# Class keys only of blocks outside the local scores, counted in the local masks; five products on a constant fewer; a fixed order at four other places

## The chip, the cores and the metric

The kernel runs on one core of one Trainium2 chip, in one launch. The metric is the device time of that launch in microseconds (us). A core has a matrix engine (TensorE, PE in the profile, with its weight loads as PEld), a vector engine (VectorE, DVE), an activation engine (ScalarE, ACT), a general engine (GpSimd, POOL) and a sync engine (SP) that issues the DMA transfers. Each engine works through its own queue in order; semaphores hold an instruction back until what it reads is there.

## The reference

One decoder layer on x of 1024 tokens by 1024 features, float32, with two mixers whose outputs are concatenated:

```python
h = rmsnorm(x, norm1_w)
proj = h @ w_in
# mixer A: gated delta rule, 4 heads of 128, gated by silu(z)
# mixer B: dilated attention, 8 heads of 64
DIL_PATTERNS = ((128, 1), (512, 4), (2048, 16))
...
for window, dil in DIL_PATTERNS:
    # query t sees keys t, t-dil, ..., t-window
    num, den, m = band_attention(stride(qf), stride(kf), stride(vf), window // dil)
...
out = num_tot / den_tot            # branches weighted by their softmax denominators
...
x = x + concat([o_a, o_b]) @ w_out
h = rmsnorm(x, norm2_w)
u = causal_dwconv(h @ w_up, ffn_conv_w)
x = x + (silu(gate) * up) @ w_down
return rmsnorm(x, final_norm_w)
```

The merge of the three attention branches amounts to one softmax over all keys of the query, in which a key that several branches see counts as often as they see it. Branch 1 sees the last 128 tokens. Branches 2 and 3 see only keys whose distance is a multiple of 4 (up to 512) or of 16.

## The kernel before, in words

Float32 matrices are split into a rounded high part and the rest (a low part), and a product of two of them is three products: high by high, high by low, low by high (`mm3`, L196, "a group" below). ACT makes the high part, DVE the low part (`split`, L202). Everything lies transposed: features or weights on the partitions, tokens along the row.

A planner writes the program: streams of work (`wv.add`, L1603) yield their estimated due times, and `Weave.run` decides in which order PE's products are recorded. PE keeps that order. On the other engines a scheduler orders what is recorded; `after(inst, anchor)` (L185) fixes that one instruction stands behind another, and `uv` and `ua` are DVE and ACT with a higher priority.

- **Start (L261 to L346).** Eighteen products on a constant tile `warm` come first (L332). Then `first()` computes three column blocks of the input projection: for each k of eight feature blocks, six groups (three blocks by two token halves). A tile of x per k is loaded, split into `xhi` and `xlo`, squared and summed into `acc` for the first norm. For k = 0 the tile comes in two halves, and the groups take all three blocks of one half first. Weights for two k at a time are loaded and split (`whi`, `wlo`); the adds for the norm stand in the same DVE queue.
- **Mixer A (to about 300 us)** and the rest of the input projection (`dense`, L486): 16 groups per column block, eight for each token half, with the result scaled by `rstdB` into `xr` or `aqkv` by DVE. The dense groups fill PE between the steps of the other streams. The z columns come last; `gate` (L463) makes silu(z) times the mixer's output `og` from them.
- **Attention (L879 to L1036).** Two heads (e = 0, 1, on 64 partitions each) at a time make a head pair, `pi` = 0 to 3; eight query blocks n of 128 tokens each, in pairs: (0, 1), (2, 3), (4, 5), (6, 7). Inside a block, tokens are ordered by class, that is, by position modulo 4. For a block, `scores` computes *local scores*, against its own and the previous block (128 columns for n = 0, 256 otherwise), and *class scores*: each of the four classes against the keys of the same class, of `nb` blocks of class keys, 128 columns per `nb`. `nb` is 1 for n < 4 and 2 from n = 4 on. A class product has 32 stationary columns, so four classes and two heads make eight per block. Masks from the tiles `mks` add a large negative number, or the logarithm of the count, to each column; a row's exponentials and sum follow (`normalise`, L930). `turn` transposes the probabilities on PE, 128 columns at a time; DVE copies the local part to `pt`, ACT the class part to `pb`. `values` multiplies by local values, and `merge_classes` (L975), once for four blocks, by class values: for each class, class-key block and head one product of 128 columns (four blocks of 32 queries). `give` copies the result `oT` out. The pairs are pipelined by one: a pair's scores are recorded before the values of the pair before it.
- **Output projection (L1073).** Its products start when attention is over and the last z is gated; `mixer_splits` splits `og` into `ohi`, `olo`.
- **Up projection (L1187 to L1320).** Seven half-size products P1 to P7 per step instead of eight, for 22 steps. P1, P6, P7 and P4 add up in one bank `pa`, of which ACT takes copies on the way (`p1`, `u2`, `u3`), so that the next product waits for the copy. In the first step the second norm is also computed: row sums on PE, a power on POOL (`rms2_power`, L1171), transposes of the result and a copy to `rstdB` (`rms2_spread`, L1180).
- **Down projection (L1326 to L1601).** Stages 0 to 3 of 11 steps each; each step's operands are prepared one or two steps ahead (`prep`, L1384, DVE's part in `lows`), ACT and DVE in the order written down (`keep`, L1351). In stage 3 the right half of the tokens is already done and is normed (`final_norm`, L1517: row sums, `rs`, a power on POOL, four transposes, eight scalings with their output transfers); its two steps `down_step(3, 4)` and `(3, 5)` lie between the row sums and the transposes. The last five steps are run column block by column block in products of 256 columns, so that the left half's norm can be done in two quarters.

Of the kernel before, what the change touches and what calls it, by code (L numbers as in the profile page):

```python
# [144 lines left out]
def hybrid_layer(tc, I, out):  # L145
# [126 lines left out]

    for k in range(KT):
# [24 lines left out]
        sq = A("sq", "qa")  # L298
        ac.activation(sq, xt, AF.Square)
        if k == 0:  # L300
            sq0 = sq
        elif k == 1:
            ve.tensor_tensor(acc, sq0, sq, op=OP.add)
        else:
            inst = ve.tensor_tensor(acc, acc, sq, op=OP.add)
            if k == 6:
                after(inst, first_lo, "the products wait for these weights")
        if k == 4:
            first_lo = wlast

# [21 lines left out]
    for _ in range(18):  # L332
        mm(wbank[:, :P], warm, warm, 0.3)
# [129 lines left out]
    def gate(og, xr, anchor=None):  # L463
# [3 lines left out]
                 ve.tensor_tensor(og, og, y, op=OP.mult)]  # L467
        if anchor is not None:
# [409 lines left out]

    def attention():  # L879
# [11 lines left out]
        def mask(n):  # L891

            i, o, step, w, m = {0: (0, 128, 352, 128, 2), 1: (1, 0, 128, 128, 3), 2: (1, 384, 128, 128, 3),
                                3: (0, 608, 128, 128, 3)}.get(n, (0, 0, 480 - 32 * n, 256, 2))
# [3 lines left out]
        def scores(pair):  # L898
# [76 lines left out]
        def merge_classes(g):  # L975
# [41 lines left out]
        for pi in range(4):  # L1017
            q, k, vn, vc = cur
            for hh in range(2):
# [9 lines left out]
                for u in (0, 2):  # L1029
                    more = att_values(qkv[2]) if (hh, u) == (1, 2) and pi < 3 else None  # L1030
                    yield from advance([dict(n=4 * hh + i, u=i, q=q, k=k, vn=vn, nb=nb, po=po, pb=pb, g=g)
# [16 lines left out]
    def mixer_splits():  # L1048
# [4 lines left out]
        for i in range(8):  # L1053
            yield from wv.until(("o", i))
            ots[i] = (X("ohi"), X("olo"))
            if i < H:
                split(gated[i], *ots[i])
# [79 lines left out]
    def split_block(b, src):  # L1137
        ac.activation(b[0], src, AF.Copy)
        return ve.tensor_tensor(b[1], src, b[0].bitcast(F32), op=OP.subtract)

    def residual(m):
# [11 lines left out]
        else:  # L1153
# [8 lines left out]
            split_block(hblock("T4", i), b21)  # L1162
            split_block(hblock("B22", i), b22)
        for h in range(2):
# [6 lines left out]
    def rms2_power():  # L1171
# [4 lines left out]
        ve.tensor_scalar(rs, ps[:, :NCH], 1.0 / 1024, EPS, op0=OP.mult, op1=OP.add)  # L1176
# [20 lines left out]
    def up_weights(n, names):  # L1197
# [18 lines left out]
        if "A22" in names:  # L1216
# [7 lines left out]
            split_block(pairs[1], u)  # L1224
            for i, name in enumerate(("S3", "A12", "S4", "A22")):
# [17 lines left out]
    def up(n, before):  # L1243
# [16 lines left out]
        ac.activation(u2, pa, AF.Copy)  # L1260
# [6 lines left out]
        if before is not None:  # L1267
# [3 lines left out]
        ac.activation(u3, pa, AF.Copy)  # L1271
# [4 lines left out]
        if before is None:  # L1276
            rms2_spread(rs)
# [239 lines left out]
    def final_norm(hh, sl, tags, between=None, more=()):  # L1517
# [9 lines left out]
        ve.tensor_scalar(rs[:, :n_], ss[:, :n_], 1.0 / 1024, EPS, op0=OP.mult, op1=OP.add)  # L1527
        rsqrt(rs[:, :n_], rs[:, :n_], n_)
        if between is not None:
            between()  # L1530
        pb = bank(tags[1])
        for c in range(n_):
            tp(pb[:, c * P:(c + 1) * P], rs[:, c:c + 1].to_broadcast([P, P]))
        for m in range(8):
            x = x1h[m][:, part(m, hh, sl)]
            ve.scalar_tensor_tensor(x, x, fw[:, m:m + 1], pb[:, :sl.stop - sl.start], op0=OP.mult, op1=OP.mult)
# [139 lines left out]
```

## Time and profile before

| | us |
|---|---|
| median of 3 timed runs | 1232.29 |
| lowest, highest | 1231.43, 1234.54 |
| profiled execution, its own time | 1235.56 |
| its span, first to last instruction | 1233.3 |
| PE busy in it | 1215.4 |

The page gives the busy time of each engine; a share near 100% for PE means that the stage's length is the sum of its products, as long as they follow on one another. Rows of groups read: line, engine, operation, out<-in, shapes, count of records | busy us, mean ns | idle time before them and what ended it. A float32 product of PE appears as two records, a transpose as one. A record's mean duration overlaps with its neighbours; busy time does not count the overlap twice. Rows of the timeline read: start, duration, engine, line, operation, out<-in, shapes, count, and in brackets the idle time of the engine before it and what ended it. Rows by stretches read: from:to, length, then busy time and count for each engine asked for, the granted clock, the DMA share and GB/s.

### The profile page before, as it was taken

The numbers are of one execution on the slowest core, as the hardware profiler recorded it, in microseconds if no ns is written. First come the engines' busy times: TensorE is split into PE (matmuls) and PEld (weight loads), VectorE is DVE, ScalarE is ACT, GpSimd is POOL, SyncE is SP. The second block draws the span as 40 slices with busy tenths as digits, with TensorE's granted clock in tenths as the row PEclk, the third lists the DMA queues.
The fourth block names the chain that finished last, engine by engine and source line by source line (L and its number), as shares of the span: only waits on it lengthen the run. The fifth ranks groups of instructions, "written<-read, shape, count | busy, mean of one in ns | idle before, by whom it ended". The sixth has DMA issues, their size and how long they took to land.

```text
span 1233.3 us, 18302 instructions
## 1 busy us (share of the span) xinstructions
PE 1215.4 (99%) x7048; PEld 1005.1 (81%) x7048; DVE 967.1 (78%) x1529; ACT 585.5 (47%) x1127; POOL 51.2 (4%) x34
## 2 busy tenths in 40 slices
PE   9999999999999999999999999999999999999996
PEld 7888887898777777888788888888888888888886
DVE  7686984473666777677789888898898979898986
ACT  7383344363444445455454454454444554445451
POOL 0212110022000000000000000000000000000001
PEclk9999999999999999999999999999999999999999
DMA  7423235337442222443331322312213296357733
GB/s 231 103 75 98 86 115 160 103 103 235 133 132 75 104 61 61 140 162 109 112 103 52 103 85 69 103 57 98 101 54 103 77 358 237 106 183 224 238 95 137
DMA packets 81702, 153.52 MB, mean 124 GB/s; under 512 B 21552, under 2 KB 32464, under 8 KB 81616
## 3 DMA queue, kind: packets, MB, share of 16 engines
q1 hardware_dynamic: 81616, 152.37, 37.9%
q8 instruction: 55, 0.90, 0.3%
q14 instruction: 31, 0.25, 0.1%
HBM read 114.31 MB, written 35.93 MB: 122 GB/s over the span
## 4 chain that ended last, share of the span: by engine, by line
PE 94%; DVE 3%; issue 1%; ACT 1%; DMA 0%; POOL 0%; POOLq 0%; DVEq 0%; ACTq 0%
PE ps L189 46%; PE pa L189 19%; PE dw L189 15%; PE pc L189 9%; PE ps L193 4%; DVE x1h L139 1%; DVE pr L139 1%; PE warm L189 1%; DMA wst<-in_wu 0%; DVE rstdB L139 0%; POOL rs L139 0%; DVE olo L139 0%; DVE pt L141 0%; DVE T L139 0%; DVE wst L139 0%
## 5 line engine op out<-in xcount | busy, mean ns | idle before, releaser
L189 PE MATMUL dw<-pr 128*128 128x512 f32 (+1 forms) x984 | 211.3, 376 | 0.0
L189 PEld LDWEIGHTS dw<-pr 128*128 128x128 f32 x984 | 176.6, 188 | 33.6
L189 PE MATMUL ps<-xhi,whi 128*128 128x512 f32 x448 | 187.0, 417 | 0.0
L189 PE MATMUL ps<-xhi,wlo 128*128 128x512 f32 x448 | 176.1, 393 | 0.0
L189 PE MATMUL ps<-xlo,whi 128*128 128x512 f32 x448 | 175.4, 391 | 0.0
L189 PE MATMUL pa<-T,pair 128*128 128x512 f32 x528 | 127.1, 390 | 2.2 <-ACT u L139 2.2
L189 PEld LDWEIGHTS pa<-T,pair 128*128 128x128 f32 x528 | 98.9, 188 | 23.2 <-ACT u L139 2.7
L189 PEld LDWEIGHTS ps<-xhi,wlo 128*128 128x128 f32 x448 | 84.3, 188 | 18.6
L189 PEld LDWEIGHTS ps<-xhi,whi 128*128 128x128 f32 x448 | 84.5, 189 | 17.1 <-issue 3.3
L189 PEld LDWEIGHTS ps<-xlo,whi 128*128 128x128 f32 x448 | 84.8, 189 | 13.2
L139 ACT ACTIVATE u<-pa 128x512 f32<-128x512 f32 x44 | 26.3, 598 | 108.6 <-PE pa L189 108.6
L139 DVE SCALAR_TENSOR_TENSOR y<-xu,fcw,y 128x1023 f32<-128x1023 f32 (+1 forms) x44 | 56.4, 1281 | 24.4 <-ACT y L139 24.4
L139 ACT ACTIVATE pr<-wd 128x1024 fp32r<-128x1024 f32 x33 | 35.0, 1061 | 76.9 <-DVE wd L139 38.2
L139 ACT ACTIVATE whi<-wst 128x1024 fp32r<-128x1024 f32 (+2 forms) x38 | 38.5, 1014 | 60.0 <-PE ps L189 49.8
L189 PE MATMUL pa<-B,A 128*128 128x512 f32 x264 | 63.5, 389 | 0.0
L189 PE MATMUL pc<-B,pair 128*128 128x512 f32 x264 | 63.4, 389 | 0.0
L189 PE MATMUL pc<-T,S 128*128 128x512 f32 x264 | 63.4, 389 | 0.0
L189 PE MATMUL pa<-T,S 128*128 128x512 f32 x264 | 63.4, 389 | 0.0
L141 ACT ACTIVATE sm<-sm,mx 128x512 f32<-128x512 f32 (+2 forms) x64 | 41.2, 646 | 42.2 <-DVE mx L141 42.2
L139 DVE TENSOR_TENSOR wst<-wst 128x512 f32<-128x512 f32 x88 | 60.3, 686 | 0.7
L189 PE MATMUL ps<-B,pair 128*128 128x512 f32 x252 | 60.5, 389 | 0.0
L189 PEld LDWEIGHTS pa<-T,S 128*128 128x128 f32 x264 | 49.5, 188 | 10.3
(233 smaller groups left out, 2312.5 us busy)
## 6 DMA issues: line engine op xcount, KB each, us to landing
wst<-in_wu SPq DMA_DIRECT2D x44, 512.0 KB, 3.7
wd<-in_wd SPq DMA_DIRECT2D x44, 512.0 KB, 4.4
wst<-in_wi SPq DMA_DIRECT2D x25, 512.0 KB, 3.7
upark<-y SPq DMA_DIRECT2D x22, 512.0 KB, 3.7
r<-upark SPq DMA_DIRECT2D x22, 512.0 KB, 9.3
apark<-aqkv SPq DMA_DIRECT2D x12, 512.0 KB, 2.8
wa<-in_wd SPq DMA_DIRECT2D x22, 256.0 KB, 3.0
wst<-in_wo SPq DMA_DIRECT2D x8, 512.0 KB, 4.1
```

The costliest lines, as they stand in the source:

```text
L139: return getattr(eng, op)(*a, **kw)
L141: return getattr(eng, op)(*a, **kw)
L189: tc.stamp_issue_order_token(nc.tensor.matmul(dst, lhs, rhs, start=start, stop=stop, **kw).ins, TOKEN)
L193: tc.stamp_issue_order_token(nc.tensor.transpose(dst, src, ident).ins, TOKEN)
```

## The change

- **Class keys.** `CBLOCKS` gives each query block its own `nb`: 0 for blocks 0 and 1, 1 for blocks 2 to 5, 2 for blocks 6 and 7. Where a class key lies inside the local 256 columns only, it is no longer a column of its own; the local mask counts how often the three branches see it. The masks are laid out anew. Blocks 0 and 1 have no class scores, no class probabilities and one transpose less per head; blocks 4 and 5 have 128 class columns less. `merge_classes` leaves the blocks without a class-key block out of its products (64 columns instead of 128).
- **Start.** Thirteen products on the constant instead of 18. The x tile of k = 1 is loaded and split in two halves, its groups take one half first, and the squares of a tile are recorded after the split of the next.
- **End of attention.** The gate products and low parts of mixer A's outputs are ordered behind the last copies of probabilities and the low parts of the first output weights.
- **First steps of the up projection.** The copies `u2` and `u3` are ordered ahead of some splits; `rms2_spread` is recorded between P7 and P4 instead of after P4; the sum's scaling has the higher priority.
- **Stage 3 of the down projection.** `rs` and a copy of it behind the power stand in the written DVE order, one step earlier; one step lies between the row sums and the transposes, the other behind them; the eight scalings are ordered behind the last step's low parts.
- **Last norm.** Two of the scalings are ordered behind the adds of the last two column blocks.

```diff
+    def squares(k):
+        sqs[k] = A("sq", "qa")
+        ac.activation(sqs[k], xts[k], AF.Square)
+        if k == 1:
+            ve.tensor_tensor(acc, sqs[0], sqs[1], op=OP.add)
+        elif k > 1:
+            inst = ve.tensor_tensor(acc, acc, sqs[k], op=OP.add)
...
-            sy.dma_start(xt, I["xT"][k * P:(k + 1) * P, :])
+            parts = [half(0), half(1)] if k == 1 else [slice(0, S)]
+            for sl in parts:
+                sy.dma_start(xt[:, sl], I["xT"][k * P:(k + 1) * P, sl])
...
-            split_x(xt, k, slice(0, S))
+            for sl in parts:
+                split_x(xt, k, sl)
+            squares(k - 1)
...
-    for _ in range(18):
+    for _ in range(13):
         mm(wbank[:, :P], warm, warm, 0.3)
...
-            for i in range(6) if k else (0, 2, 4, 1, 3, 5):
+            for i in range(6) if k > 1 else (0, 2, 4, 1, 3, 5):
...
+    CBLOCKS = (0, 0, 1, 1, 1, 1, 2, 2)
...
-                for c in range(4):
+                for c in range(4 if it["nb"] else 0):
...
-            if it["g"]["pi"] == 3 and it["n"] > 5:
-                for lo in last.get("wlo", ()):
+            if it["g"]["pi"] == 3 and it["n"] == 7 and e == 1:
+                lows = last.get("wlo", [])
+                last["probabilities"] = inst
+                for lo in lows:
                     after(lo, inst, "the probabilities go first")
-            ua.activation(it["pb"][e][:, it["u"]].rearrange("p b t -> p (b t)"), pp[:, n1_:wd], AF.Copy)
+                for slow in last["og"] + last.get("olo", [])[1:]:
+                    after(slow, (lows or [inst])[0], "the first weights go first")
+            if it["nb"]:
+                ua.activation(it["pb"][e][:, it["u"], :it["nb"]].rearrange("p b t -> p (b t)"), pp[:, n1_:wd], AF.Copy)
...
+                    us = slice(2 if b == nb - 1 else 0, 4)
                     for e in range(2):
                         er = slice(64 * e, 64 * e + 64)
-                        mm(po[er].rearrange("p (u t) -> p u t", u=4)[:, :, 32 * c:32 * c + 32],
-                           vcv[:, c, b, er], g["pb"][e][:, :, b, 32 * c:32 * c + 32], 0.14,
+                        mm(po[er].rearrange("p (u t) -> p u t", u=4)[:, us, 32 * c:32 * c + 32],
+                           vcv[:, c, b, er], g["pb"][e][:, us, b, 32 * c:32 * c + 32], 0.14 if us.start == 0 else 0.08,
...
+                if i and "probabilities" in last:
+                    after(lo, last["probabilities"], "the probabilities go first")
...
-        ve.tensor_scalar(rs, ps[:, :NCH], 1.0 / 1024, EPS, op0=OP.mult, op1=OP.add)
+        uv.tensor_scalar(rs, ps[:, :NCH], 1.0 / 1024, EPS, op0=OP.mult, op1=OP.add)
...
+            if n == 1:
+                after(last["hi"], last["u3"], "the next product waits for the copy")
...
-        ac.activation(u2, pa, AF.Copy)
+        inst = ac.activation(u2, pa, AF.Copy)
+        if before is None:
+            for hi in last["lasts"]:
+                after(hi, inst, "the next product waits for the copy")
...
         yield from up_product(n, "P7", pa, False, False)
-        if before is not None:
+        if before is None:
+            rms2_spread(rs)
+        else:
             pd = yield from next_bank("hf")
...
         rsqrt(rs[:, :n_], rs[:, :n_], n_)
+        if hh:
+            keep("vector", inst)
+            rp, rs = rs, tile_(sp, [P, 4], F32, "rs3", "rs3", 2)
+            keep("vector", ve.tensor_copy(rs, rp))
...
-                def two_steps():
-                    down_step(3, j)
-                    prep(3, j + 3)
-                    down_step(3, j + 1)
-                final_norm(1, whole, ("hf", "ch"), two_steps)
-            elif stage < 3 or j < HT - LAST - 1:
+                outs = final_norm(1, whole, ("hf", "ch"), lambda: down_step(stage, j))
+            elif stage < 3 or j < HT - LAST:
                 down_step(stage, j)
+        for inst in outs:
+            after(inst, prev["vector"], "the last steps' weights go first")
...
+        after(outs[4], adds[2, right.start], "the last norm waits for it")
+        after(outs[7], adds[3, right.start], "the last norm waits for it")
...
-    p1 = np.where((d >= 0) & (d <= 128), 0.0, NEG)
+    def logs(mult):
+        return np.where(mult > 0, 8.0 * np.log(np.maximum(mult, 1)), NEG)
+    local = logs(((d >= 0) & (d <= 128)).astype(int) + ((d >= 0) & (d % 4 == 0)) + ((d >= 0) & (d % 16 == 0)))
```

More of the change, by code (lines that the diff above doesn't have):

```diff
@@ L271, in split_x @@
                                 op1=OP.subtract)
+    def squares(k):
[5 more added lines that the diff above has]
+            inst = ve.tensor_tensor(acc, acc, sqs[k], op=OP.add)
+            if k == 6:
+                after(inst, first_lo, "the products wait for these weights")
+    sqs = {}
     for k in range(KT):
@@ L293, in hybrid_layer @@
                 sy.dma_start(wst, I["w0"][k // 2])
-            sy.dma_start(xt, I["xT"][k * P:(k + 1) * P, :])
+            parts = [half(0), half(1)] if k == 1 else [slice(0, S)]
+            for sl in parts:
+                sy.dma_start(xt[:, sl], I["xT"][k * P:(k + 1) * P, sl])
             if k % 2 == 0:
                 wlast = split(wst, whi, wlo)
-            split_x(xt, k, slice(0, S))
[L298 to L307, printed above, removed]
+            for sl in parts:
+                split_x(xt, k, sl)
+            squares(k - 1)
         if k == 4:
             first_lo = wlast
+    squares(KT - 1)
     ident = const("ident", [P, P], I["ident"])
@@ L467, in gate @@
                  ve.tensor_tensor(og, og, y, op=OP.mult)]
+        last["og"] = insts[2:]
         if anchor is not None:
@@ L1056, in mixer_splits @@
             if i < H:
-                split(gated[i], *ots[i])
+                lo = split(gated[i], *ots[i])
+                last.setdefault("olo", []).append(lo)
+                if i and "probabilities" in last:
+                    after(lo, last["probabilities"], "the probabilities go first")
             else:
@@ L1275, in up @@
         ac.activation(xu[:, half(0)], pa, AF.Copy)
-        if before is None:
-            rms2_spread(rs)
         def rest():
@@ L1591, in last_product @@
                 down(pa[i], i, ops[3, j][0], sl, False, j == HT - 1)
-            add_to(pa[i], 4 + i, 0, sl)
+            adds[i, sl.start] = add_to(pa[i], 4 + i, 0, sl)
             return complete(4 + i, 0, sl, alone)
@@ L1599, in mlp_down @@
         last_product(0, right)
-        final_norm(0, left, ("hf", "ch"), lambda: last_product(1, right))
-        final_norm(0, right, ("hf", "ch"), more=[last_product(i, right, True) for i in (2, 3)])
+        outs = final_norm(0, left, ("hf", "ch"), lambda: last_product(1, right))
+        squares = [last_product(i, right, True) for i in (2, 3)]
+        after(outs[4], adds[2, right.start], "the last norm waits for it")
+        after(outs[7], adds[3, right.start], "the last norm waits for it")
+        final_norm(0, right, ("hf", "ch"), more=squares)
     wv.add(0, norms())
```

32 lines of the change are left out of this document (19 added, 13 removed).

## The prediction

> **What bounds the kernel now.** I read the busy time by engine first, then the list of who waited for whom on TensorE (PE).
>
> ```profile
> PE 1215.4 (99%) x7048; PEld 1005.1 (81%) x7048; DVE 967.1 (78%) x1529; ACT 585.5 (47%) x1127; POOL 51.2 (4%) x34
> ...
> PE ps L193 <- POOL rs L139: 2.3, 2, 1.2
> ```
>
> PE lacks 17.9 us of the 1233.3 us span. A removed product is therefore worth its full time wherever PE does not stand waiting at that place; work taken from VectorE (DVE) or ScalarE (ACT) is worth nothing by itself. The list of waits is short (its longest entry is above: microseconds in all, times, the longest); those that the new orders touch are quoted at their parts. In the attention stage the same is seen by stretches (sums per engine in one stretch of time):
>
> ```profile
> 375.00:420.00 45.00, 45.00 (x434) 35.54 (x433) 30.82 (x81) 18.90 (x53) 0.00 (x0) 1.00 0.32 105
> ```
>
> PE is busy all 45.00 us, DVE 30.82 of them.
>
> **Part 1, the start.** Thirteen products on a constant are issued instead of 18; each is two records. PE by stretches over those records, then the rows that limit what follows:
>
> ```profile
> 1.10:6.10 5.00, 4.99 (x23) 1.00 0.65 175
> 6.10:7.54 1.44, 1.44 (x15) 1.00 0.90 237
> ...
> 5.21 0.75 DVE L139 SCALAR_TENSOR_TENSOR xlo<-xt,n,xhi 128x512 fp32r<-128x512 f32 x1 [0.50 <-ACT xhi L139]
> 8.78 0.56 DVE L139 TENSOR_TENSOR wlo<-wst,whi 128x384 fp32r<-128x384 f32 x1 [0.61 <-ACT whi L139]
> 10.31 1.28 DVE L139 SCALAR_TENSOR_TENSOR xlo<-xt,n,xhi 128x1024 fp32r<-128x1024 f32 x1 [0.97 <-ACT xhi L139]
> 23.17 0.95 DVE L139 TENSOR_TENSOR wlo<-wst,whi 128x768 fp32r<-128x768 f32 x1
> 24.43 0.39 PE L189 MATMUL ps<-xhi,wlo 128*128 128x512 f32 x1
> ```
>
> Of the 36 records 23 fall in the first 5.00 us (0.22 us each); the 13 left take 1.44 us, 0.11 us each. The ten that go come from the fast end: 10 x 0.11 = 1.1 us, not ten times the mean of 6.44/36 = 0.18. [...]
>
> The operands are there: the low part of the first half of x ends at 5.96, and PE would now ask at 7.54 - 1.1 = 6.4. The next limit is the low weights of k=4. DVE works without a pause from 10.31 to 24.12, when they end, and PE reads them at 24.43, a margin of 0.31. With the second x tile in halves, DVE can begin it at about 9.4 (after the row at 8.78). The order of squares and the halves then cost it about 0.35, and the load of the gate weights, now behind a weight load in the sync queue, perhaps 0.2. So those weights come at about 23.6 and PE asks at 23.3: 0.3 is lost, and I take 0.8. Bounds: 0 and 1.1.
>
> **Part 2, class keys.** Groups of records by form:
>
> ```profile
> L189 PE MATMUL ps<-kT,qT 64*32 64x256 f32 x256 | 8.8, 382 | 0.0
> L189 PE MATMUL ps<-kT,qT 64*32 64x128 f32 x256 | 5.3, 275 | 0.0
> L189 PE MATMUL ps<-pb,vc 128*64 128x128 f32 x192 | 12.0, 273 | 0.0
> L189 PE MATMUL ps<-kT 128*128 128x128 f32 x64 | 8.4, 274 | 0.0
> L189 PE MATMUL ps<-ones,rstdB 128*128 128x1 f32 x32 | 4.0, 245 | 1.1 <-DVE rstdB L139 1.1
> ...
> 463.61 0.82 PE L193 MATMUL ps<-ident,sm 128*128 128x128 f32 x6
> 464.18 0.47 PE L189 MATMUL ps<-xhi,whi 128*128 128x512 f32 x1
> 476.19 1.03 PE L193 MATMUL ps<-ident,sm 128*128 128x128 f32 x8
> 476.99 0.48 PE L189 MATMUL ps<-xhi,whi 128*128 128x512 f32 x1
> ```
>
> Sixteen class products (32 records) with 256 keys take 8.8/8 = 1.10 us, with 128 keys 5.3/8 = 0.66. Per head pair, query blocks 0 and 1 lose one set of 0.66, and blocks 4 and 5 go from 1.10 to 0.66. That is 1.10 per head pair, 4.4 in all.
>
> Six transposes take 0.57 us and eight 0.80: 0.11 for one more. Blocks 0, 1, 4 and 5 each lose one per head, eight per head pair, 32 in all: 3.5 us.
>
> The products of class probabilities on class values keep their number (24 per head pair); 16 of them stream 64 columns instead of 128. A product with one column costs 4.0/32 = 0.125 us, nearly as much as one with 128 columns, 8.4/64 = 0.131; what is paid is the stationary operand, which is unchanged here. I take 0. The other bound: 128 records x 12.0/192 = 8.0 us, halved, 4.0.
>
> The shorter score reductions, exponentials and copies lie under PE. Part 2 is 7.9 us.
>
> **Part 3, the end of attention.** PE stands before these three:
>
> ```profile
> 491.40 0.43 PE L189 MATMUL ps<-pt,vn 128*64 128x128 f32 x2 [0.82 <-DVE pt L141]
> 492.86 1.20 PE L189 MATMUL ps<-pt,vn 128*64 128x128 f32 x13 [1.03 <-DVE pt L141]
> 498.58 0.50 PE L189 MATMUL ps<-ohi,whi 128*128 128x512 f32 x1 [0.39 <-DVE oT L139]
> ```
>
> These are 2.24 us. The copies of the probabilities came behind gate products and low parts on DVE. Now those stand behind the copies, and six groups of z products stand between the merge and the output projection and cover oT. What is late next is the first output bank, which must wait for the scaling of the last z half: about 0.1. The last gate (two ACT and three DVE steps plus that scaling, some 6.5 us) is needed only after 36 products, 8.2 us. Gain 2.1; bounds 0.5 and 2.24.
>
> **Part 4, start of the up product.**
>
> ```profile
> 594.59 1.84 PE L189 MATMUL ps<-ones,rstdB 128*128 128x1 f32 x16
> 597.19 3.06 PE L189 MATMUL pa<-T,pair 128*128 128x512 f32 x12 [0.76 <-ACT u L139]
> 601.65 3.01 PE L189 MATMUL pa<-T,pair 128*128 128x512 f32 x12 [1.41 <-ACT u L139]
> 604.50 1.04 PE L193 MATMUL ps<-ident,rs 128*128 128x128 f32 x8
> 605.29 2.99 PE L189 MATMUL pa<-B,A 128*128 128x512 f32 x12
> ...
> 596.56 0.58 ACT L139 ACTIVATE u<-pa 128x512 f32<-128x512 f32 x1
> 598.77 0.16 DVE L139 TENSOR_SCALAR rs<-ps 128x8 f32<-128x8 f32 x1
> 599.01 2.06 POOL L139 TENSOR_TENSOR rs<-rs,mhalf 128x8 f32<-128x8 f32 x1 [300.35 <-DVE rs L139]
> ```
>
> Both waits on ACT go: u2, which began at 596.56, moves ahead of two splits of 0.53 each and is ready at about 596.1, before the row sums end at 596.43, and u3 ahead of the split it was queued behind. But the eight transposes of rs move to right behind P7, which now ends at about 599.2. In the changed DVE queue rs still stands behind five splits and sums, so it comes at about 598.6; GpSimd (POOL) then needs 2.06, and PE gets rs at about 601.0. So PE waits 1.8 us at a new place. Then 0.8 of transposes and 2.7 of P4: the second pass begins at 604.6 instead of 605.29. Gain 0.7, not 2.17. Queued behind on DVE is a copy of rstdB with the sums for xu and xg; the next pass needs them microseconds later. Bounds: 0 and 2.17. [...]
>
> **Part 5, the last norms.**
>
> ```profile
> 1199.17 5.69 PE L189 MATMUL dw<-pr 128*128 128x512 f32 x24
> 1206.06 0.65 PE L193 MATMUL ps<-ident,rs 128*128 128x128 f32 x4 [1.19 <-POOL rs L139]
> 1206.46 9.24 PE L189 MATMUL dw<-pr 128*128 128x256 f32 x75
> 1216.55 0.61 PE L189 MATMUL ps<-ones,rstdB 128*128 128x1 f32 x4 [0.85 <-DVE rstdB L139]
> ...
> 1201.61 4.40 POOL L139 TENSOR_TENSOR rs<-rs,mhalf 128x4 f32<-128x4 f32 x1 [600.53 <-DVE rs L139]
> 1217.43 0.70 POOL L139 TENSOR_TENSOR rs<-rs,mhalf 128x2 f32<-128x2 f32 x1 [11.43 <-DVE rs L139]
> 1206.75 5.36 DVE L139 SCALAR_TENSOR_TENSOR x1h<-x1h,fw,ps 128x512 f32<-128x512 f32 x8 [1.61 <-PE ps L193]
> 1222.89 0.74 DVE L139 TENSOR_TENSOR x1h<-x1h,dw 128x256 f32<-128x256 f32 x2
> ```
>
> DVE now takes rs one pair of low parts sooner (1200.2 for 1201.38) and waits for POOL at the copy behind it. POOL then has no busy DVE beside it: 0.7 to 1.4 us, I take 1.0. DVE stalls about 1.3; PE transposes between its two steps of 12 products without waiting and reaches the half-width products at 1199.17 + 2.72 + 0.4 + 2.72, about 1205.1, instead of 1206.46. The four pairs of low parts end at about 1206.4, just before PE reads the last of them. The eight scalings start 0.25 earlier; the adds behind them no longer wait for PE, and the row sums at 1216.55 come about 1.2 us earlier. The two adds at 1222.89 move up between the scalings before them, behind the last of which both stood; the last square begins some 0.45 sooner. Part 5: 1.65; bounds 0.4 and 2.2.
>
> **Sum.** 0.8 + 7.9 + 2.1 + 0.7 + 1.65 = 13.15 us. The profiled execution took 1235.56 us (1233.3 of span, 2.3 around it), so this makes 1222.4 there; it lies 3.3 above the median of the runs, 1232.29, and the forecast is 1232.29 - 13.15 = 1219.1 us.
>
> **Rivals.**
>
> (a) Products with half the columns cost half. For it: 256 against 128 class keys is 1.10 against 0.66. Against: the one-column row. 4.0 more, 1215.1 us. Chance 0.12.
>
> (b) The new wait of part 4 does not come (rs is early enough): 1.5 more, 1217.6. For it: it is the reorder's plain reading; against: the DVE queue. Chance 0.12.
>
> (c) Attention's softmax chain becomes the bound in part of the stage: half of part 2 returns as PE waits, 1219.1 + 4 = 1223.1. For it: the margin of the first block pair is small (rows below, 0.35 us), and the changed order has fewer groups of filling products in some gaps. Against: DVE has 14 us in 45 to spare, and its steps shorten with the keys. Chance 0.15.
>
> (d) The other side: in every pair of blocks the transposes wait for the divisions.
>
> ```profile
> 451.40 0.62 DVE L141 TENSOR_SCALAR sm<-sm,mx 128x256 f32<-128x256 f32 x2
> 452.37 0.66 PE L193 MATMUL ps<-ident,sm 128*128 128x128 f32 x4
> ```
>
> The division ends at 452.02 and PE reads it at 452.37. PE will come 0.66 sooner; the chain shortens by four reductions and two exponentials of 128 columns less, about 0.7. Were it not to shorten, 0.3 us would be lost at this pair. The kernel is slower once the mean loss over the 16 pairs passes 13.15/16 = 0.82 us; at 1.0 it is 1219.1 + 16 = 1235.1. Against: in the stretch of 45 us above no pair waited at all. Chance 0.03.
>
> (e) A new order only moves its wait at the ends (parts 1, 3, 4 and 5 at their lower bounds, 4.35 less): 1223.5. Chance 0.08.
>
> **How the numbers follow.** The forecast, with 1217.2 to 1221.2 around it, has 0.50. All parts at their small ends give 1232.29 - 8.8 = 1223.5, and with some of (c) 1225; at their large ends 1232.29 - (1.1 + 11.9 + 2.24 + 2.17 + 2.2) = 1212.7, which needs (a) and (b) together. I take 1214.5 to 1225. A measurement of this kernel tells about 0.3%, 3.7 us, from no change: faster 0.95, the same 0.02, slower 0.03, nearly all of the last being (d).
>
> **What would show it.** Part 1: 13 products, the first real one at about 6.4, a short PE wait near 23 for wlo. Part 2: no products of 32 keys' columns for blocks 0 and 1, 184 transposes instead of 216, class-value products of 64 columns still near 0.06 us a record, and a head pair's period about 42.8 us instead of 44.8. Part 3: no PE wait for pt or oT. Part 4: none for u, but 1.8 us for POOL rs. Part 5: a power of about 1 us, no wait for rs, a span's end some 1.6 us nearer to the last full-width product. The prediction is wrong if PE shows gaps before ps<-ident,sm in the head pairs, or if the class-value products fall to half.

## The result, and the profile after

| | before | after |
|---|---|---|
| median of 4 timed runs, us | 1233.28 | 1220.85 |
| lowest, highest | 1231.43, 1234.54 | 1219.62, 1222.42 |
| profiled execution, its span | 1235.56, 1233.3 | 1219.62, 1217.6 |

The ratio is 0.989, with a 95% interval of 0.9876 to 0.9905: the change saves 11.7 to 15.3 us, 12.4 by the medians. The forecast was 1219.1 us, 13.15 saved.

First the page of the changed kernel, the line of busy times, and below it its list of who waited for whom on PE (microseconds in all, times, the longest):

```profile
PE 1202.1 (99%) x6878; PEld 995.2 (82%) x6878; DVE 962.3 (79%) x1531; ACT 576.2 (47%) x1112; POOL 48.0 (4%) x34
...
PE ps L193 <- POOL rs L139: 3.0, 2, 2.0
PE warm L189 <- DVE ones L139: 1.1, 1, 1.1
PE ps L189 <- DVE rstdB L139: 0.8, 1, 0.8
PE ps L189 <- ACT pb L141: 0.8, 1, 0.8
PE ps L189 <- issue: 0.6, 1, 0.6
PE ps L189 <- ACT w L141: 0.5, 1, 0.5
PE ps L189 <- DVE wlo L139: 0.4, 1, 0.4
PE ps L189 <- DVE pt L141: 0.3, 1, 0.3
```

PE's busy time fell by 13.3 us, its idle time from 17.9 to 15.5. The waits for u and oT are gone and pt is down to 0.3; new are 2.0 for POOL rs (one of the two entries of 3.0), 0.8 for pb, 0.4 for wlo. To see where the 15.7 us between the two profiled spans lie, take the start of one recurring PE row at the border of each stage in both timelines and subtract:

| stretch, from the row before to this row | before | after | saved | forecast |
|---|---|---|---|---|
| start to the first norm's row sums (ones,acc) | 30.73 | 30.42 | 0.3 | 0.8 |
| to the first scores (kT,qT) | 281.57 | 279.30 | 2.3 | 0 |
| to the second norm's row sums (first ones,rstdB) | 282.29 | 270.65 | 11.6 | 10.0 (7.9 + 2.1) |
| to the second pass of the up product (B,A) | 10.70 | 10.41 | 0.3 | 0.7 |
| to the row sums of the first of the last norms | 593.07 | 592.96 | 0.1 | 0 |
| to the row sums of the next | 18.19 | 16.81 | 1.4 | 1.65 for the three |
| to the last transposes of rs | 9.46 | 8.96 | 0.5 | |
| to the end | 7.3 | 8.1 | -0.8 | |

The 2.3 us of the second row lie in code that the change does not touch. Two things make them: a PE wait named "issue" of 1.4 us in the one execution and 0.6 in the other, and a stretch of 3.41 us at half the clock that only the profiled execution of before has (last section). Without them 13.4 us are left, close to the 13.15, but the terms differ from those of the sum.

The start, in the timeline of the changed kernel (start, duration, ..., in brackets the idle time before and what ended it):

```profile
1.11 5.70 PE L189 MATMUL warm<-warm 128*128 128x128 f32 x26 [1.11 <-DVE ones L139]
6.57 0.48 PE L189 MATMUL ps<-xhi,whi 128*128 128x512 f32 x1
...
20.26 1.14 ACT L139 ACTIVATE xhi<-xt,n 128x1024 fp32r<-128x1024 f32 x1
21.30 0.83 ACT L139 ACTIVATE whi<-wst 128x768 fp32r<-128x768 f32 x1
...
23.00 0.95 DVE L139 TENSOR_TENSOR wlo<-wst,whi 128x768 fp32r<-128x768 f32 x1
24.00 0.50 PE L189 MATMUL ps<-xhi,wlo 128*128 128x512 f32 x1 [0.39 <-DVE wlo L139]
```

The first real product starts at 6.57 instead of 7.54, 0.97 earlier, nearly what ten fast records allow (1.1). But the low weights of k=4 end at 23.95, only 0.17 earlier than before, and PE gives most of it back there.

Inside a head pair, the scores of two blocks and, behind two blocks' values, the class-value products; before, then after:

```profile
375.59 2.16 PE L189 MATMUL ps<-kT,qT 64*128 64x256 f32 x40
377.67 1.09 PE L189 MATMUL ps<-pt,vn 128*64 128x128 f32 x16
378.60 1.04 PE L189 MATMUL ps<-pb,vc 128*64 128x128 f32 x16
```

```profile
367.91 1.73 PE L189 MATMUL ps<-kT,qT 64*128 64x256 f32 x40
369.57 1.09 PE L189 MATMUL ps<-pt,vn 128*64 128x128 f32 x16
370.49 0.64 PE L189 MATMUL ps<-pb,vc 128*64 128x64 f32 x16
```

The scores lose 0.43 us, as reckoned (0.44). The sixteen class-value records lose 0.40, where the forecast had nothing.

### The profile page after: what moved, and what is told of

Same layout as the page of the kernel before. It is cut to its first block, busy times and chain, and to the rows that moved or that the text cites. A ratio compares the mean times of both kernels' runs of the same rounds, so it can differ in the third digit from the quotient of the medians.

```text
span 1217.6 us, 17960 instructions
## 1 busy us (share of the span) xinstructions
PE 1202.1 (99%) x6878; PEld 995.2 (82%) x6878; DVE 962.3 (79%) x1531; ACT 576.2 (47%) x1112; POOL 48.0 (4%) x34
## 4 chain that ended last, share of the span: by engine, by line
PE 90%; DVE 4%; DMA 2%; issue 1%; ACT 1%; POOL 0%; SPq 0%; POOLq 0%; DVEq 0%; ACTq 0%
PE ps L189 44%; PE pa L189 19%; PE dw L189 14%; PE pc L189 10%; PE ps L193 3%; DVE x1h L139 1%; DVE pr L139 1%; DMA wst<-in_w 1%; DMA wst<-in_wu 1%; DVE rstdB L139 0%; DVE sm L141 0%; DMA xt<-in_xT 0%; DMA wst<-in_wo 0%; POOL rs L139 0%; DMA wba<-in_wba 0%
## 5 line engine op out<-in xcount | busy, mean ns | idle before, releaser
L141 ACT ACTIVATE sm<-sm,mx 128x384 f32<-128x384 f32 (+3 forms) x64 | 37.8, 592 | 45.5 <-DVE mx L141 45.5
```

The lines of the kernel that those rows point to most:

```text
L141: return getattr(eng, op)(*a, **kw)
```

## The experiments

**Part 2 alone.** The kernel before with the edits of the class keys (`CBLOCKS`, masks, fewer class scores and transposes, halved class-value products) and nothing else:

```diff
+    CBLOCKS = (0, 0, 1, 1, 1, 1, 2, 2)
...
-                for c in range(4):
+                for c in range(4 if it["nb"] else 0):
...
+                    us = slice(2 if b == nb - 1 else 0, 4)
```

> The kernel before with part 2 alone (class keys counted in the local masks; starts, ends and norms as before). Theory A (the halved class-value products are worth their columns): a head pair's period falls from 44.8 to about 42.1 us once moved filling products are set aside (1.10 of scores, 0.88 of transposes, 0.71 of class values), 10.6 us in all. Theory B (the prediction's own step: halved products are worth nothing): 1.98 us for each head pair, 7.9 in all. Theory C (softmax comes back as a wait): TensorE waits before the transposes of sm inside the head pairs, and less than 6 in all. Either way the waits at the end of attention (pt 1.9, oT 0.4), for u (2.2), and the contended power of 4.4 us in the last norm stay.

Median 1222.57 us against 1234.61, ratio 0.9904 (0.9887 to 0.9922). From the first scores to the second norm's row sums it takes 271.16 us in place of 282.29, 11.1 saved, about 10.7 by the rows of the head pairs (2.69 for each, below) and the rest at the end of attention, where, against the expectation, the wait for oT went and pt fell. PE's longest waits in it:

```profile
PE ps L193 <- POOL rs L139: 2.3, 2, 1.2
PE pa L189 <- ACT u L139: 2.1, 2, 1.4
PE ps L189 <- DVE pt L141: 1.3, 2, 1.0
PE ps L189 <- DVE rstdB L139: 1.1, 2, 0.8
```

No PE wait for sm appears there or further down that list, so theory C falls. A head pair's period is 41.4 us as it stands, in this kernel and in the full change; the filling products have to be set aside. Over one period, the products on high weights (columns: from:to, length, PE busy with these instructions and their number, ...) of before and of the full change are:

```profile
366.10:410.90 44.80, 22.20 (x68) 11.88 (x68) 2.64 (x3) 3.05 (x3) 1.00 0.23 72
```

```profile
358.40:399.83 41.43, 21.60 (x66) 11.49 (x66) 2.42 (x2) 2.10 (x2) 1.00 0.28 89
```

Two of three products in a group read high weights, so there are 33 groups in place of 34. One group, 0.68 us, is pushed out of each period and done after the last one: moved, not saved. The true saving is 44.80 - 41.43 - 0.68 = 2.69 us for each head pair (theory A: 2.69; theory B: 1.98).

**The disputed term by itself.** The kernel before, where 16 of a head pair's 24 class-value products leave out 64 of their 128 columns (so a part of the attention output is missing):

```diff
+                    us = slice(2 if b == nb - 1 else 0, 4)
...
-                        mm(po[er].rearrange("p (u t) -> p u t", u=4)[:, :, 32 * c:32 * c + 32],
+                        mm(po[er].rearrange("p (u t) -> p u t", u=4)[:, us, 32 * c:32 * c + 32],
```

> The kernel before, but 16 of a head pair's 24 products of class probabilities on class values stream only the upper 64 columns of their 128; the contribution of the other 64 columns is left out. Scores, transposes and softmax as before. Theory A (columns are paid): a run of 16 records goes from 0.77 to about 0.41 us from first to last start, 32 records from 1.64 to 1.29, 0.71 us for each head pair, 2.8 us in all. Theory B (what is paid is the stationary operand, as the prediction took it): the runs of records keep 0.77 and 1.64, gain 0. Rival (a) of the prediction: exactly half of each record, 1.0 for each head pair, 4.0 in all.

And with 32 columns in place of 64:

```diff
-                    us = slice(2 if b == nb - 1 else 0, 4)
+                    us = slice(3 if b == nb - 1 else 0, 4)
```

> As the kernel before with 64 of 128 columns in 16 of a head pair's 24 class-value products, but with 32 columns; the contribution of the other 96 is left out. If columns are paid all the way down, 16 records go to about 0.20 us from first to last start (0.0137 us a record). If at 64 columns the load of the stationary operand of 64 columns is already the limit, they stay at 0.41 (0.027 a record). If the limit lies between, in between.

The row of sixteen records with 64 columns, then with 32 (one run, 1233.48 us, with two stretches at half the clock, see the last section):

```profile
377.04 0.63 PE L189 MATMUL ps<-pb,vc 128*64 128x64 f32 x16
```

```profile
379.05 0.61 PE L189 MATMUL ps<-pb,vc 128*64 128x32 f32 x16
```

From first to last start (15 intervals) sixteen records take 0.77 us with 128 columns, 0.41 with 64, 0.38 with 32. How they do it stands in the starts of the single records: the two heads' records start 7 ns apart, side by side, and one such pair follows the pair before by 0.109 us with 128 columns, by 0.058 with 64 (0.056 for the first) and, but for a first step of 0.028, by 0.058 with 32 too. So 64 columns are paid nearly in full, and at 64 a floor begins: 32 fewer gain only that one first step. That is the second case of the expectation above. The forecast took its floor from `ones,rstdB`, whose records start 0.112 us apart with one column; its stationary operand has 128 columns, here it has 64, and two heads share each step. By these starts the floor is 0.058 us for a pair with 64 stationary columns and about twice that, 0.112, for a record with 128; the loads of the two heads' stationary operands start 7 ns apart as well, so they are not paid one after the other. That the load makes the floor is my estimate from these sizes, since no run changed the stationary columns alone.

As a whole, the kernel with 64 columns ran 1230.04 us against 1234.61, ratio 0.9964 (0.9951 to 0.9977). Its attention took 278.91 us, 3.4 less, although the class-value rows alone lost 2.8 and the waits for pt (1.9 to 0.2) and oT (0.4) all but went. About 1.5 came back: a wait for sm of 0.3, and the records of some score groups spread (the last one takes 2.14 us from first to last start instead of 1.78; one of its records waits for an ACT copy to pb). That is rival (c) in small: with the same softmax and less for PE to do, its chain is late in places. With the masks of the change only one execution of eleven shows such a wait, 0.2 us; that it is rarer because reductions and exponentials shrink with the keys is likely, but no run separates it.

**The order at the up product.** The changed kernel with the transposes of rs behind P4 again:

```diff
-            rms2_spread(rs)
-        else:
...
         ac.activation(xu[:, half(0)], pa, AF.Copy)
+        if before is None:
+            rms2_spread(rs)
```

> The changed kernel with one of its moves undone: the eight transposes of rs stand behind P4 again; the early copies u2 and u3 stay. Theory (the 2.0 us wait for POOL rs is the price of the move): no wait for rs or for u at the start of the up product, row sums to the second pass 0.4 + 10.4 - 2.0, so about 8.4 us in place of 10.4, and 2.0 us less than the changed kernel, about 1218.9. Rival 1 (rstdB comes later and the first pass's products on it run late): TensorE waits for xu, y or the next tiles some microseconds later, and less than 0.5 is gained. Rival 2 (P4's own operands or the bank of xu are not ready that early): a wait before P4 of 1 us or more.

Median 1218.27 us against 1234.61, ratio 0.9873 (0.9855 to 0.9891). The changed kernel's timeline, then that of this one:

```profile
580.36 1.84 PE L189 MATMUL ps<-ones,rstdB 128*128 128x1 f32 x16
582.09 3.00 PE L189 MATMUL pa<-T,pair 128*128 128x512 f32 x12
587.08 1.09 PE L193 MATMUL ps<-ident,rs 128*128 128x128 f32 x8 [2.00 <-POOL rs L139]
587.93 3.01 PE L189 MATMUL pa<-T,pair 128*128 128x512 f32 x12
590.77 2.88 PE L189 MATMUL pa<-B,A 128*128 128x512 f32 x12
...
584.72 0.16 DVE L141 TENSOR_SCALAR rs<-ps 128x8 f32<-128x8 f32 x1
584.96 2.06 POOL L139 TENSOR_TENSOR rs<-rs,mhalf 128x8 f32<-128x8 f32 x1 [288.89 <-DVE rs L141]
```

```profile
585.50 3.01 PE L189 MATMUL pa<-T,pair 128*128 128x512 f32 x12 [0.75 <-ACT u L139]
588.35 1.03 PE L193 MATMUL ps<-ident,rs 128*128 128x128 f32 x8
```

The wait for rs goes, one for u of 0.75 returns: the transposes had covered the copy u3. From row sums to second pass it is 9.06 us in place of 10.41, 1.35 saved of the 2.0 expected. So the wait for rs is the price of the move, but the move also pays 0.75; rival 2 named the place, with 1 us or more. The wait is not always 2.0: in the six executions with this part as changed it is 0.9 to 2.0, mean 1.5, and the stretch 9.26 to 10.41, mean 9.8. Against that mean 0.8 is saved here, and 0.9 by the next variant.

**rs earlier, the transposes where they are.** On DVE the sum for rs is put ahead of the low parts of T4 and B22 and of a weight sum:

```diff
-        uv.tensor_scalar(rs, ps[:, :NCH], 1.0 / 1024, EPS, op0=OP.mult, op1=OP.add)
+        inst = uv.tensor_scalar(rs, ps[:, :NCH], 1.0 / 1024, EPS, op0=OP.mult, op1=OP.add)
+        for slow in last["late"][-2:]:
+            after(slow, inst, "the sums go first")
...
-            split_block(hblock("T4", i), b21)
+            late(split_block(hblock("T4", i), b21))
```

> The changed kernel, with the sum for rs put ahead of four sums and splits that stand before it on VectorE at the start of the up product (low parts of T4 and B22, a weight sum, low part of S). Transposes stay between P7 and P4. Theory A (rs was late on VectorE, not on GpSimd): the sum runs at the end of the row sums, 2.3 us earlier than in the changed kernel; the power of 2.06 us ends before P7 does; no wait for POOL rs, none for u (the transposes cover the copy u3); row sums to second pass 8.4 us in place of 10.4; 2.0 us less than the changed kernel. Theory B (something else of the path is as late): a wait of 0.5 us or more stays at the transposes, or a new one comes at the second pass because two copies of rstdB now stand ahead of the pair sums; gain below 1.

One run, 1217.04 us. Its timeline:

```profile
582.19 2.04 POOL L139 TENSOR_TENSOR rs<-rs,mhalf 128x8 f32<-128x8 f32 x1 [286.27 <-DVE rs L141]
586.10 3.02 PE L189 MATMUL pa<-T,pair 128*128 128x512 f32 x12 [0.48 <-ACT u L139]
```

The power takes 2.04 us as before, but starts 2.1 us behind the first row sum instead of 4.6, and ends before P7 does. So rs was late on DVE, as the forecast had it, and not on POOL. A wait for u of 0.48 stays (u3 stood behind a split of pair weights on ACT); 8.89 us from row sums to second pass, 1.5 saved against the execution shown above.

**The start.** The weights of k=4 ahead of x tile 5 on ACT and DVE:

```diff
+        if k == 5:
+            after(inst, highs_made[-1], "these weights go first")
...
+        if k == 5:
+            after(inst, first_lo, "these weights go first")
```

> The changed kernel, with the weights of k=4 ahead of x tile 5 on ScalarE (high part) and VectorE (low part). Theory A (these low weights are what limits the start): wlo of k=4 is made 0.9 us or more earlier, no wait for wlo near 23; the first product at about 6.6 as in the changed kernel, and all of the 0.97 us kept at 40 us (the changed kernel kept 0.3). Theory B (x tiles come as late): a wait for xlo of k=5 near 27, or for the next weights, of the same 0.4 to 0.7 us, and nothing gained.

One run, 1217.59 us. Its low weights on DVE:

```profile
21.42 0.95 DVE L139 TENSOR_TENSOR wlo<-wst,whi 128x768 fp32r<-128x768 f32 x1
```

They end at 22.37 instead of 23.95, and no wait for wlo or xlo is listed. The row sums of the first norm begin at 29.30 us. In three executions with this order it is 29.14 to 29.30; in seven with the start as changed 29.61 to 31.00, mean 30.5; in four with the start of before 30.73 to 31.32, mean 30.95. So part 1 is worth 0.5 on average, and 1.7 with the weights first. Not all of the difference is the order: the clock became whole at 4.6 to 5.1 us in these three and at 4.8 to 7.0 in the seven (6.45 in the first profile of the changed kernel), and the first product started at 5.8 and 6.2 on average. From the first product to the row sums it is 23.4 and 24.3 us, so the order itself is worth about 0.9.

**All orders together**, with the last copies of class probabilities ahead of the high parts of gated values on ACT (a wait for pb of 0.8 at the end of attention):

```diff
+                    for hi in last.get("ohi", []):
+                        after(hi, inst, "the probabilities go first")
```

> The changed kernel with three orders in addition: rs first on VectorE, weights of k=4 first at the start, and the last four copies of class probabilities ahead of the high parts of gated values on ScalarE. Theory: waits for POOL rs (2.0), ACT pb (0.8) and DVE wlo (0.4 to 0.8) all go, 3.2 us or a little more below the changed kernel in the same set of runs. Rival for the third order: TensorE then waits as long for pt, or the first output product waits for ohi; then 0.8 less is gained. If orders only move waits: less than 1 us.

> The changed kernel once more, beside the variant with three orders on the same chip. Expected 12 to 13.5 us below before; waits for POOL rs near 2.0 at the start of the up product and 1.0 at the end, ACT pb 0.8; the start between 0 and 1 us ahead of before. The time from the last scaling's start to the end, 7.6 us in its first profile and 6.85 in that of before: if the 0.76 belongs to the change it is 7.6 again, if it is a matter of the execution it is nearer to 6.9.

1215.61 us against 1220.80 for the changed kernel on the same chip (there the wait for POOL rs was 1.3, not near 2.0 as expected, and the late end of 7.6 us came back as 7.7); ratios to before 0.9854 (0.9837 to 0.9871) and 0.989 (0.9875 to 0.9905). That is 5.2 us, more than the 3.2 expected. By the borders of the stages the start gives 1.2, attention 1.0 and the up product 0.8. Most of the rest of the 6.9 us between the two spans is again the stretch near 205 us (2.9), and the end (1.0).

**u3 first as well:**

```diff
             split_block(pairs[0], g)
+            if n == 1:
+                after(last["hi"], last["u3"], "the next product waits for the copy")
```

> The variant with three orders and a fourth one: the copy u3 stands ahead of the first pair split too on ScalarE (with rs first, it was 0.48 us late behind that split). Theory: the wait for u goes as well, row sums to second pass 8.4 us in place of 8.87, 0.5 us less than with three orders (1215.6 in the runs before), so about 1215.1. Rival: the pair split, now 0.6 us later, delays the pair sums on VectorE and P5 to P7 of the second pass; nothing gained.

```profile
582.26 1.03 PE L193 MATMUL ps<-ident,rs 128*128 128x128 f32 x8
583.17 3.01 PE L189 MATMUL pa<-T,pair 128*128 128x512 f32 x12
586.02 2.88 PE L189 MATMUL pa<-B,A 128*128 128x512 f32 x12
```

No wait is left there: 8.27 us from row sums to second pass, 0.6 less. The median is 1215.48 us against 1234.78, ratio 0.9854 (0.9837 to 0.9870). 0.6 us is less than such runs can tell; this place of the timeline shows it. By its ratio to before this version is ahead of the changed kernel (0.989), and level with all three orders.

**The last norms.** The changed kernel without the copy of rs behind which DVE waits:

```diff
         if hh:
             keep("vector", inst)
-            rp, rs = rs, tile_(sp, [P, 4], F32, "rs3", "rs3", 2)
-            keep("vector", ve.tensor_copy(rs, rp))
```

> The changed kernel without the copy of rs behind which VectorE waits for GpSimd in the first of the last norms; the order of steps stays the changed one. Theory A (the copy keeps VectorE off GpSimd's power): the power takes about 4.4 us again instead of 1.0, TensorE stands some 3 us before the transposes of rs (after one step of 12 products instead of two), and row sums to row sums of the next norm goes from 16.81 to 19 or 20 us, above the 18.19 of the kernel before. Theory B (the gain of part 5 is the order of steps): 16.8 to 17.3 us, and no wait of over 1 us for rs there.

First POOL and PE of the changed kernel, then of this one (1227.13 us, one run):

```profile
1185.78 1.01 POOL L139 TENSOR_TENSOR rs<-rs,mhalf 128x4 f32<-128x4 f32 x1 [598.75 <-DVE rs L139]
1187.35 0.60 PE L193 MATMUL ps<-ident,rs 128*128 128x128 f32 x4
```

```profile
1186.52 5.60 POOL L139 TENSOR_TENSOR rs<-rs,mhalf 128x4 f32<-128x4 f32 x1 [598.72 <-DVE rs L139]
1192.17 1.11 PE L193 MATMUL ps<-ident,rs 128*128 128x128 f32 x4 [3.92 <-POOL rs L139]
```

The same power on 128x4 takes 1.01 us while DVE stands still, and 5.60 while DVE adds (4.40 in the kernel before). PE waits 3.92, and from row sums to row sums it takes 23.31 us instead of 16.81. That is above the 19 to 20 expected, since the power was longer and PE had half the clock for 6.8 us, from 1.7 us before the wait ended. The order of steps without the copy is a loss: theory A.

How the additions delay it, the traces show in part: in all five executions with a slow power (4.40 us in four, 5.60 here) a DVE addition had started 0.16 us before it, and the power ended 0.87 us behind the last of an unbroken row of additions, as if it had run only then. But the power on 128x8 at the up product, also begun just behind a DVE addition, took 2.01 to 2.07 us in all fourteen, and with the transposes behind P4 it ended before the additions did; why the two differ stays open.

**The end.** The changed kernel without the two orders of the last additions, run twice:

```diff
-        after(outs[4], adds[2, right.start], "the last norm waits for it")
-        after(outs[7], adds[3, right.start], "the last norm waits for it")
```

> The changed kernel without the two orders that put the last two additions between the scalings of the norm before. Theory of the prediction: the last norm's row sums to its transposes of rs go from 8.96 back to about 9.46 us (0.5 us lost). For the time from the last write's issue to the end (2.97 us in four executions with the order of before, 3.0 to 3.8 in six with the changed one): if the two orders make the last write late, it is 2.97 here; if not, it may be anything from 3.0 to 3.8.

> The same kernel as the one without the two orders of the additions, once more, as a second sample of the time from the last write's issue to the end: 2.97 again if the two orders are the cause.

1218.31 and 1220.14 us. Row sums to last transposes take 9.40 us in both (8.96 with the orders), 0.44 lost, as the forecast had it. From the issue of the last write to the end it is 3.75 and 3.95 us. So the two orders are not what makes the last write late. In four executions with the end of before that time was 2.95 to 2.97, in ten with a changed end 3.0 to 3.95. The traces of all fourteen narrow it down. In six (the two of the changed kernel, the one with the weights of k=4 first alone, the one without the copy, and both of this variant) the last two writes take 2.65 to 3.04 us to land, in the other eight 1.86 to 1.90. In those six one transfer of 8 KB on a queue that loads instructions starts 2.9 to 3.0 us before the end, among these writes; in the eight others the last such transfer starts 0.3 to 1.9 us behind the last instruction. The changed kernel's queues from 1213 to 1216 us:

```profile
q14 instruction: 1, 0.01, 1.0%
```

So the late end goes with a load of code that falls among the last writes. The six are also those in which the transposes of rs wait for POOL at the up product; how an order there moves the load was not found, and no run moved the load alone.

## Why the prediction was right, point by point

- **Part 1 (0.8): too large.** The ten records gave 0.97 at the first product. The step that failed is "those weights come at about 23.6". They came at 23.95: I had shifted DVE's queue as a whole, but x tile 5 stands ahead of them on both engines, and with the new order of squares ACT makes its high part 0.5 us later than before (20.26, quoted above, for 19.73), so that DVE waits for it. Much of what the start wins is lost there. 0.3 in the profiled execution, 0.5 on average.
- **Part 2 (7.9): too small, about 10.7.** Scores and transposes came as reckoned (1.10 and 0.88 for each head pair). The failed step is "what is paid is the stationary operand, which is unchanged here. I take 0": the halved records gave 0.71 for each head pair, 2.8 in all, of the 4.0 of rival (a). The rows compared were records with 128 stationary columns, called products there, 0.112 us from start to start; with 64, and two heads side by side, a pair's floor is 0.058. The prediction's own last sign, "if the class-value products fall to half", came true.
- **Part 3 (2.1): too large, about 1.1.** pt (1.85 to 0.3) and oT (0.39 to 0) went as said. Part 2 alone already took oT's wait and a part of pt's; the orders added about 0.5 to it (271.16 to 270.65 us). "What is late next" was not the first output bank but pb: ACT did high parts of gated values between copies of class probabilities, and PE waited 0.8. I had followed DVE's queue only. With the copies first, the wait goes (row sums 0.8 to 1.3 us earlier in two executions).
- **Part 4 (0.7): right.** The new wait for POOL rs is there, 2.0 for the 1.8 forecast (0.9 to 2.0 in six executions). Saved are 0.3 in the profiled execution; six with this part as changed take 9.26 to 10.41 us, mean 9.8, three with that of before 10.11 to 10.70, mean 10.5: 0.6. A fourth with that of before, with 32 columns, took 11.96, at half the clock in part, and is left out. Rival (b) falls.
- **Part 5 (1.65): right, and hidden.** Power of 1.01, row sums 1.4 earlier, last norm 0.5: 1.9. The later landing of the last writes took 0.8 of it in the profiled execution; the forecast had nothing for it.
- **Rivals.** (a) in mechanism: the halved products do pay, two thirds of its price. (c) and (d): of eleven executions with the masks of the change only one, the second of the two without the orders of the last additions, has a wait for sm, 0.2 us. (e): the ends of parts 1 and 3 moved their waits in part.

The forecast of 1219.1 is 1.75 us from the median. That is less than the terms were off in the profiled execution: part 2 was 2.8 too small, parts 1, 3 and 4 together 1.9 too large, and 0.8 was lost at the end. These errors have opposite signs and nearly cancel; so far the closeness is luck. A stretch of 3.41 us at half the clock, in code that no version changed, adds to the difference of the two profiled executions.

## What to carry to other kernels

A floor read from one row holds for the shape of its stationary operand (here 0.112 us for a record with 128 stationary columns, 0.058 for a pair with 64), and for records that follow on one another; before a term is set to nothing by it, look for a row with the same stationary columns, and at the starts of single records. When an order is changed for one engine, follow every engine's queue to the next reader: three of the waits met here (wlo, pb, u) came from ACT's queue. And a POOL power that takes 1.0 us beside an idle DVE took 4.4 and 5.6 beside an unbroken row of DVE additions; making DVE wait for it was the cheaper order here (16.81 us in place of 23.31 from row sums to row sums).

## What the runs showed of the hardware

At one place PE had half its clock for 3.41 us after it had idled for part of the 3.41 us before. By stretches, before and then the changed kernel's second profile (length, PE busy, granted clock, ...):

```profile
204.09:207.50 3.41, 1.96 (x66) 1.00 0.14 52
207.50:210.92 3.42, 3.42 (x54) 0.50 0.50 156
```

```profile
203.53:206.94 3.41, 2.18 (x82) 1.00 0.18 64
206.94:210.36 3.42, 3.42 (x54) 0.50 0.30 85
```

In each, PE was busy 57 and 64% of 3.41 us and then ran 3.41 us at half the clock, about 1.7 us lost. The execution with 32 columns shows the same at 207.8 us (63%), and once more at 593.5, behind one-column row sums and a wait for u. These three are the ones where PE's wait "issue" lasted 1.2 us or more; in eleven others it was 0.8 or less, and the clock stayed whole there. So at this place a wait of 1.3 us cost about 3 (281.3 to 281.6 us from the first norm's row sums to the first scores, against 278.5 to 278.7 in the four executions without the wait), and it lies in code that no version changed: the spread of single runs by some 3 us is in part this.

What the wait is, the transfers show: in ten of the fourteen executions PE stands there, 0.3 to 1.45 us, and in all ten it goes on 1.3 to 1.5 us behind the end of a 16 KB transfer on the other instruction queue (q8). Just before it PE runs through small products fast, three every 32 ns. So PE most likely waits for its code there; no run moved this load.

The busy share alone does not tell when the clock is lost. The stretch in the kernel before lasts 3.413 us, and it begins 59 times that behind 6.15 us, where the clock at the start became whole (207.53 - 6.15 is 201.38); the two with 32 columns begin 113 times that from one another (593.50 - 207.79 is 385.71). So other windows of the same grid can be compared. First a window of the kernel before in which PE was busy 53% and which was followed by the whole clock, then the second stretch of the execution with 32 columns, which 87% went before:

```profile
490.84:494.25 3.41, 1.82 (x24) 1.00 0.36 139
```

```profile
590.09:593.50 3.41, 2.95 (x22) 1.00 0.00 0
593.50:596.91 3.41, 3.41 (x9) 0.50 0.00 0
```

In the execution without the copy, a wait of 3.92 us went with 6.8 us at half the clock, the first 1.7 of them inside the wait. None of the windows before these stretches was wholly idle (PE was busy 1.25 of the 3.40 us before those 6.8), and what beside idle time counts stays open here.
